# A hybrid RWKV-7/S5 block on one core: masking the chunk matrices on VectorE, and solving the two directions' triangular systems as two series

## The chip, the core and the metric

The kernel runs on one core of a Trainium2 chip. The metric is device time in microseconds (us). The kernel before takes 2064.58 us, the median of three runs (2061.06 to 2066.1). Names used below: PE is TensorE (matmuls; PEld its weight loads), DVE is VectorE, ACT is ScalarE, POOL is GpSimd, SP is the engine whose queue issues nearly all DMAs. Each engine executes its own instructions strictly in the order in which they stand in its queue, and SP's DMAs are issued in their order as well: a DMA that waits for its data holds all that stand behind it.

## The reference, cut to what matters

The model has two layers. Layer 0 mixes the tokens (256 context tokens and 512 latent ones, 768 in all) with eight bidirectional RWKV-7 heads and, beside them, 32 S5 groups; layer 1 uses latent attention; each layer ends in a mixture of experts. The change touches layer 0's mixer alone. Its core is this recurrence, for both directions z and each head:

```python
def _rwkv_step(S, inp):
    r, w, k, v, kk, a = inp
    sa = jnp.einsum('zbhvk,zbhk->zbhv', S, kk)
    S = S * w[..., None, :] - sa[..., None] * (a * kk)[..., None, :] + v[..., None] * k[..., None, :]
    return S, jnp.einsum('zbhvk,zbhk->zbhv', S, r)
```

After it each token's output is normalised per head, gets a bonus term and a gate, and is concatenated with the S5 output; then `o_l = cat @ w_out` follows. The per-layer modulation rows (`silu(c) @ mod_w[layer] + mod_b[layer]`) are a separate product over 25 MB of weights for each layer.

## The kernel before, in words

The recurrence is computed in chunks of 64 tokens. The six tiles of 128 tokens are visited in six turns s = 0 to 5 (forward direction in one order, backward in another), and each turn has two steps of one chunk for each direction. Four pieces of code make up a turn, called in `rwkv` (line 1841 and on):

- **Stage a** (`rwkv_stage_a`) loads a turn's r, k and normalised k (`rk`, from `qbuf` and `kkd`), evaluates decay and gate polynomials on ACT, POOL and DVE (`sg`, `ta`, `vv`, `ev`, `od`), scans the decays on DVE (`E`), and forms the operands `PQ` and `KB` on DVE, `ev` and `ta` products on POOL. Its last DVE instruction is `KB<-ta,E` of the second direction.
- **Stage b** (`rwkv_stage_b`) forms the chunk matrices. Per direction z and chunk parity par, PE multiplies `KB` with `PQ` into two PSUM tiles `pg`; ACT copies them to `G` in SBUF (line 570), POOL multiplies `G` with the triangular mask `gmask` (line 571). The 16x16 diagonal blocks go by DMA to DRAM (`nt`, 16 DMAs of 4 per z and par) and come back as rows `A` with one block per partition: 128 partitions hold 2 directions x 2 parities x 4 blocks x 8 heads. On them DVE inverts all blocks by forward substitution: 15 rounds of two instructions, `xt<-X,A` and `X<-X,xt`, 30 in a chain in which each needs the one before (lines 589 to 592). The inverse goes out (`xo`) and back (`D`, 16 DMAs). PE and ACT then merge 16-blocks into 32-blocks (`pd`, with the DVE addition `G<-D,pd`, 8 instructions) and into 64-blocks (`pt`, `Tb`, ACT `G<-pt`).
- **Steps** (`rwkv_steps`) run the chunk recurrence: PE products `pU`, ACT copies `R` and `VU`, PE `pZ` and `pY`, DVE scales the state (`Z<-Z,dc`) and adds (`Z<-pZ,Z`, two instructions per step). `Y` goes to DRAM as `yd`.
- **S5 runs** (`s5_run`, 16 of them in eight pairs, `S5N` says how many pairs stand behind each turn): a table `s5tq` is loaded, PE forms `s5S`, DVE rotates and scans (`s5t`, `s5G`), POOL rotates back (`s5t`, `s5H`), PE forms `s5y`, ACT and DVE apply the activation (`s5g`, `zt`); after each second pair the gate follows (`s5zT`). `s5t` and `s5G` have one buffer each.

The calls stand in the order steps(s), stage b(s+1), stage a(s+2), S5 pairs. The framework's list scheduler places all instructions at build time: what was written earlier has priority, an instruction takes its place in an engine's queue when the scheduler's own clock finds its inputs ready. `G`, `KB`, `VU` and the operand tiles have two or three buffers, `A`, `X`, `xt`, `D16`, `W16` one.

From turn 3 on, other work joins. `rwkv_out` finishes the output tiles 0 and 1 (written in turn 3), 3 and 4 (turn 4), 2 and 5 (turn 5): gate product `pgate`, POOL `vo<-vo,bsum` and `vo<-vo,lnb`, DVE `yo<-yo,yo` (the two directions added), statistics, and three more products, then a store to `rwbuf`; its buffers exist once, so one tile follows another. `mod_part(1, q)` computes layer 1's modulation rows for q = 0, 1, 2: 16 weight tiles `mw` of 512 KB each, three buffers, PE `psmod` into one PSUM tile, which DVE reads (`mo`) before the next q starts. The buffers of both lie where stage a's pool was, which is closed after stage a(5) is done. Behind the loop, `concat` reads `rwbuf` back (`cy`), PE transposes it (`ptcat`), and the output projection (`po`, weights `wo`) starts; its PSUM comes free when the last `pgate` has been read.

## Time and profile before

| | |
|---|---|
| median of three runs | 2064.58 us (2061.06 to 2066.1) |
| the profiled execution: time, span | 2061.18 us, 2059.5 us |
| granted TensorE clock, mean | 0.857 |
| PE, PEld, DVE, ACT, POOL busy | 79%, 56%, 61%, 37%, 38% of the span |

The profile is one execution, recorded by hardware. "Busy" is the time in which an engine had at least one instruction under way; two that overlap count once. The page divides the span in 40 slices; the loop described above takes from about 340 us to 900 us, slices 7 to 18, where none of the engines is busy throughout:

```profile
PE   3688996667777857648798999948899998789993
DVE  3799825895767765434654655485567754566544
ACT  4221324332533523212313545423445433326552
POOL 0576804662553541101524234360314233414432
```

### The profile page before, as it was taken

The page shows a single profiled execution, that of the slowest core. Times are in us where ns is not written, and L with a number is a line of the kernel's source. Part 1 is how long each engine was busy: PE and PEld are TensorE (multiplying, and loading weights), DVE is VectorE, ACT ScalarE, POOL GpSimd, SP SyncE. Part 2 cuts the span into 40 slices and gives each one's busy share as a digit, 9 for nine tenths or more (in the row PEclk, how much of TensorE's full clock was granted, in tenths as well). Part 3 has the DMA queues.
Part 4 walks back from the last instruction along what each step waited for, and adds up shares of the span by engine and source line. Part 5 has one row for each costly group of instructions (what it writes and reads, how often), then busy time and mean ns, then how long its engine had stood idle before and what let it go on. Part 6 is the DMA issues. An engine that isn't in the chain of part 4 may idle for free. (4 is left out here: it accounts for less than half of the span.)

```text
span 2059.5 us, 32386 instructions
## 1 busy us (share of the span) xinstructions
PE 1634.8 (79%) x12499; PEld 1156.0 (56%) x12499; DVE 1252.1 (61%) x2353; ACT 768.6 (37%) x1374; POOL 775.8 (38%) x732
## 2 busy tenths in 40 slices
PE   3688996667777857648798999948899998789993
PEld 2376766556666744326666666547445544666662
DVE  3799825895767765434654655485567754566544
ACT  4221324332533523212313545423445433326552
POOL 0576804662553541101524234360314233414432
PEclk9698998558867967768899999969799999899997
DMA  8654697532323227775615999860000005539974
GB/s 233 190 170 149 201 284 206 152 97 71 110 57 110 79 73 217 232 233 183 250 42 172 388 360 352 287 203 3 0 0 0 1 1 221 230 103 353 387 238 174
DMA packets 232581, 350.79 MB, mean 170 GB/s; under 512 B 57794, under 2 KB 178552, under 8 KB 217576
## 3 DMA queue, kind: packets, MB, share of 16 engines
q1 hardware_dynamic: 208944, 297.89, 43.3%
q0 software_dynamic: 10080, 44.04, 6.0%
q10 hardware_dynamic: 13400, 6.75, 1.2%
q8 instruction: 100, 1.64, 0.3%
q14 instruction: 57, 0.47, 0.1%
HBM read 280.60 MB, written 68.03 MB: 169 GB/s over the span
## 5 line engine op out<-in xcount | busy, mean ns | idle before, releaser
L163 PE MATMUL psmod<-mw,cst 128*32 128x256 f32 x768 | 79.9, 488 | 50.1 <-DMA mw<-in_mod_w_dram 49.6
L1754 PE MATMUL po<-P,vv 128*64 128x512 f32 x192 | 99.3, 622 | 0.8 <-ACT P L1751 0.4
L189 PE MATMUL pwi<-aT,wih 128*128 128x512 f32 (+1 forms) x224 | 83.0, 372 | 12.0 <-DVE q L329 12.0
L1751 ACT ACTIVATE P<-st 128x512 f32<-128x512 f32 x96 | 57.2, 597 | 94.3 <-PE st L1749 92.6
L571 POOL TENSOR_TENSOR G<-G,gmask 128x1024 f32<-128x1024 f32 x24 | 59.6, 2486 | 80.9 <-ACT G L570 80.7
L191 PE MATMUL pwi<-aT,wil 128*128 128x256 f32 (+1 forms) x224 | 81.4, 364 | 0.0
L190 PE MATMUL pwi<-aT,wih 128*128 128x256 f32 (+1 forms) x224 | 81.2, 363 | 0.0
L1079 PE MATMUL s5y<-s5tq,s5H 128*96 128x128 f32 x256 | 54.7, 365 | 30.5 <-POOL s5H L1071 19.9
L1760 POOL TENSOR_TENSOR sum<-sum,P 128x512 f32<-128x512 f32 x48 | 62.4, 1301 | 41.3 <-ACT P L1751 41.1
L1758 POOL TENSOR_TENSOR sum<-P,P 128x512 f32<-128x512 f32 x16 | 20.7, 1313 | 140.3 <-ACT P L1751 140.3
L1382 POOL DMA_INDIRECT xg<-fbuf,rk x36 | 37.5, 1043 | 94.5 <-PE ptx L229 56.7
L163 PEld LDWEIGHTS psmod<-mw,cst 128*32 128x32 f32 x768 | 19.8, 123 | 91.8 <-DMA mw<-in_mod_w_dram 67.2
L183 ACT ACTIVATE xT<-ptx 128x512 fp32r<-128x512 f32 x72 | 41.2, 596 | 66.7 <-PE ptx L229 66.3
L567 PE MATMUL pg<-PQ,KB 64*128 64x128 f32 x384 | 53.5, 365 | 14.2 <-ACT ta L496 9.7
L1079 PEld LDWEIGHTS s5y<-s5tq,s5H 128*96 128x96 f32 x256 | 43.7, 225 | 36.1 <-POOL s5H L1071 22.3
L1725 DVE TENSOR_REDUCE mxp<-sc 128x1 f32<-128x512 f32 x64 | 43.1, 685 | 29.5 <-PE sc L1724 29.0
L184 DVE TENSOR_TENSOR xT<-ptx,xT 128x512 fp32r<-128x512 f32 x72 | 48.1, 687 | 19.9 <-ACT xT L183 19.0
L189 PEld LDWEIGHTS pwi<-aT,wih 128*128 128x128 f32 x224 | 46.9, 211 | 22.7 <-issue 13.3
L567 PEld LDWEIGHTS pg<-PQ,KB 64*128 64x128 f32 x384 | 45.8, 256 | 21.8 <-ACT ta L496 10.0
L728 POOL TENSOR_TENSOR vo<-vo,bsum 128x512 f32<-128x512 f32 x6 | 6.2, 1042 | 133.3 <-DMA vo<-vtok 125.7
L229 PEld LDWEIGHTS ptx<-ident,xg 128*128 128x128 f32 x288 | 41.1, 193 | 27.1 <-issue 20.7
L229 PE MATMUL ptx<-ident,xg 128*128 128x128 f32 x288 | 43.0, 285 | 11.5 <-issue 7.0
(1564 smaller groups left out, 5258.1 us busy)
## 6 DMA issues: line engine op xcount, KB each, us to landing
mw<-in_mod_w_dram SPq DMA_DIRECT2D x96, 512.0 KB
yb<-yo SPq DMA_DIRECT2D x36, 512.0 KB
s5tq<-s5t SPq DMA_DIRECT2D x16, 960.0 KB
yb<-zrow SPq DMA_DIRECT2D x16, 512.0 KB
wi<-in_hy_w_in_dram SPq DMA_DIRECT2D x14, 512.0 KB
rk<-qbuf SPq DMA_DIRECT2D x12, 512.0 KB
fbuf<-f SPq DMA_DIRECT2D x10, 512.0 KB
s5t<-s5CP SPq DMA_DIRECT2D x4, 1152.0 KB
```

The costliest lines, as they stand in the source:

```text
L163: nc.tensor.matmul(ps[32 * j:32 * j + 32, 256 * h:256 * h + 256], self.cst[:, k, :], wt[:, j], start=(k == 0 and h == 0), stop=(k == 7), s ...
L184: nc.vector.tensor_tensor(lo, src, hi.bitcast(F32), OP.subtract)
L189: nc.tensor.matmul(out, lh, rh, start=start, stop=False, **kw)
L190: nc.tensor.matmul(out, lh, rl, start=False, stop=False, **kw)
L191: nc.tensor.matmul(out, ll, rh, start=False, stop=stop, **kw)
L229: nc.tensor.transpose(pt[:, k * 128:(k + 1) * 128], a[:, h * 4 + k::8], self.ident)
L567: nc.tensor.matmul(pg[hp][:, m], KB[rs, m, ps2], PQ[rs, m, ps2], start=True, stop=True, skip_group_check=True)
L571: nc.gpsimd.tensor_tensor(G[:, par], G[:, par], self.mask[:, z, par, None, :].to_broadcast([128, 8, 128]), OP.mult)
L1079: nc.tensor.matmul(out, H[:, g, d, k, h0:h0 + 96], CP[:, k, d, i0:i0 + 8, :].rearrange("p a b -> p (a b)"), start=False, stop=(d == 1 and ...
L1751: nc.scalar.activation(P, st, AF.Exp, scale=SCALE)
L1754: nc.tensor.matmul(po[64 * x:64 * x + 64], vv[:, kt, h0 + x, :], P, start=(kt == 0), stop=(kt == 5), skip_group_check=True)
L1760: nc.gpsimd.tensor_tensor(sums[x], sums[x], P, OP.add)
```

## The change

Four edits, all in the loop of layer 0. First, DVE multiplies `pg` in PSUM with the mask and writes `G`, in place of ACT's copy and POOL's multiplication. Second, the DRAM tiles `nt` and `xo` exist once per direction; `A` is loaded, `X` is stored and `D` fetched per direction, and each round of the substitution is two instructions on 64 partitions for each direction in place of two on 128. Third, `rwkv_stage_b` returns the last instruction of the substitution, and stage a(s+2) and the S5 pairs written behind it are traced in `tc.issue_after(...)`: their DVE instructions may not stand ahead of that last instruction in DVE's queue (other engines are not held). Fourth, S5 runs and their gate are given a priority 800 places later than they were written (`S5LATE`).

```diff
@@ -4,7 +4,7 @@
 
 
 import math
-from contextlib import ExitStack
+from contextlib import ExitStack, nullcontext
 
 import concourse.bacc as _bacc
 import concourse.bass as bass
@@ -44,6 +44,7 @@
 S5N = (1, 2, 2, 2, 1, 0, 0)
 MS14 = (4, 0, 5, 1, 6, 2, 7, 3, 12, 8, 9, 10, 11, 13)
 MODT = "lo"
+S5LATE = -800
 MODN = {3: (0,), 4: (1,), 5: (2,)}
 
 
@@ -550,9 +551,9 @@
 
         nc = self.nc
         f = lambda x: x.rearrange("p a b -> p (a b)")
-        nt, xo = (self.dr.tile([128, 256], F32, name=f"{n}{s}") for n in ("nt", "xo"))
-
-        units = [(z, par, q) for z in range(2) for par in range(2) for q in range(4)]
+        nt, xo = ([self.dr.tile([64, 256], F32, name=f"{n}{s}{z}") for z in range(2)] for n in ("nt", "xo"))
+
+        units = [(par, q) for par in range(2) for q in range(4)]
         unit = lambda d, u: dap(d, u * 8 * 256, [[16, 16], [256, 8], [1, 16]])
         for z in range(2):
             PQ, KB, dc = st[z]
@@ -567,12 +568,11 @@
                         nc.tensor.matmul(pg[hp][:, m], KB[rs, m, ps2], PQ[rs, m, ps2], start=True, stop=True,
                                          skip_group_check=True)
                 for hp in range(2):
-                    nc.scalar.activation(G[:, par, hp::2], pg[hp], AF.Copy)
-                nc.gpsimd.tensor_tensor(G[:, par], G[:, par], self.mask[:, z, par, None, :].to_broadcast([128, 8, 128]), OP.mult)
-                for u, (uz, up, q) in enumerate(units):
-                    if (uz, up) == (z, par):
-                        c = 64 - 64 * par + 16 * q
-                        nc.sync.dma_start(unit(nt, u), G[c:c + 16, par, :, c:c + 16])
+                    nc.vector.tensor_tensor(G[:, par, hp::2], pg[hp], self.mask[:, z, par, None, :].to_broadcast([128, 4, 128]),
+                                            OP.mult)
+                for q in range(4):
+                    c = 64 - 64 * par + 16 * q
+                    nc.sync.dma_start(unit(nt[z], units.index((par, q))), G[c:c + 16, par, :, c:c + 16])
             for par in range(2):
                 pt = self.psum("tp", f"pkt{z}{s}{par}", 1)
                 for m in range(4):
@@ -582,19 +582,24 @@
         A = wp.tile([128, 16, 16], F32, name=f"A{s}", tag="A", bufs=1)
         X = wp.tile([128, 16, 16], F32, name=f"X{s}", tag="X", bufs=1)
         tmp = wp.tile([128, 64], F32, name=f"xt{s}", tag="xt", bufs=1)
-        nc.sync.dma_start(f(A), nt)
-        nc.scalar.activation(X, self.xid, AF.Copy)
+        half = [slice(64 * z, 64 * z + 64) for z in range(2)]
+        for z, p in enumerate(half):
+            nc.sync.dma_start(f(A)[p], nt[z])
+            nc.scalar.activation(X[p], self.xid[p], AF.Copy)
         for r in range(15):
             m, n = r + 1, 15 - r
             tm = tmp[:, :m * n].rearrange("p (a b) -> p a b", b=n)
-            nc.vector.tensor_tensor(tm, X[:, 0:m, r:r + 1].to_broadcast([128, m, n]),
-                                    A[:, r:r + 1, m:16].to_broadcast([128, m, n]), OP.mult)
-            nc.vector.tensor_tensor(X[:, 0:m, m:16], X[:, 0:m, m:16], tm, OP.add)
-        nc.sync.dma_start(xo, f(X))
+            for p in half:
+                nc.vector.tensor_tensor(tm[p], X[p, 0:m, r:r + 1].to_broadcast([64, m, n]),
+                                        A[p, r:r + 1, m:16].to_broadcast([64, m, n]), OP.mult)
+            for p in half:
+                last = nc.vector.tensor_tensor(X[p, 0:m, m:16], X[p, 0:m, m:16], tm[p], OP.add)
         D, W = self.D16, self.W16
-        for u, (z, par, q) in enumerate(units):
-            c = 64 - 64 * par + 16 * q
-            nc.sync.dma_start(D[c:c + 16, z, :, 16 * (q % 2):16 * (q % 2) + 16], unit(xo, u))
+        for z, p in enumerate(half):
+            nc.sync.dma_start(xo[z], f(X)[p])
+            for u, (par, q) in enumerate(units):
+                c = 64 - 64 * par + 16 * q
+                nc.sync.dma_start(D[c:c + 16, z, :, 16 * (q % 2):16 * (q % 2) + 16], unit(xo[z], u))
         kw = dict(start=True, stop=True, skip_group_check=True)
 
         B = [[(32 * g, z, h) for g in range(4)] for z in range(2) for h in range(8)]
@@ -636,6 +641,7 @@
         for par in range(2):
             for z in range(2):
                 nc.scalar.activation(st[z][2][one[par], par, :, two[par]], ps[one[par], z], AF.Copy)
+        return last.ins
 
     def rwkv_state(self, rp):
         nc = self.nc
@@ -1863,19 +1869,22 @@
                 q0 = next(pairs)
                 if q0 % 4 == 0:
                     zt[0] = w5.tile([96, 8, 128], F32, name=f"zt{q0}", tag="zt", bufs=1)
-                self.s5_run(q0, zt[0], w5)
-                if q0 % 4 == 2:
-                    self.s5_glu(q0 // 4, zt[0], lambda m, z: nc.sync.dma_start(s5d[m], z), w5)
+                with self.tc.high_priority(S5LATE):
+                    self.s5_run(q0, zt[0], w5)
+                    if q0 % 4 == 2:
+                        self.s5_glu(q0 // 4, zt[0], lambda m, z: nc.sync.dma_start(s5d[m], z), w5)
 
         self.rwkv_stage_b(0, st[0], sp, gp, wp)
         s5(S5N[0])
         for s in range(6):
             self.rwkv_steps(s, st[s], wp)
+            behind = nullcontext()
             if s < 5:
-                self.rwkv_stage_b(s + 1, st[s + 1], sp, gp, wp)
-            if s < 4:
-                st[s + 2] = self.rwkv_stage_a(s + 2, sp, wa)
-            s5(S5N[s + 1])
+                behind = self.tc.issue_after(self.rwkv_stage_b(s + 1, st[s + 1], sp, gp, wp))
+            with behind:
+                if s < 4:
+                    st[s + 2] = self.rwkv_stage_a(s + 2, sp, wa)
+                s5(S5N[s + 1])
             if s in (1, 2):
                 self.zero_blocks(z0, s - 1)
             if s == 3:
```

**DVE, substitution of turn 2.** Before (left in its place among `X`, `xt`, the rows `od`, `wseg`, `E` are stage a(3), `X_5138` is turn 2's):

```order
L592 TENSOR_TENSOR X_5138<-X_5138,xt_5139 128x6x10
L513 SCALAR_TENSOR_TENSOR wseg_2691<-ev_5529,od_5535 128x8x64
L514 SCALAR_TENSOR_TENSOR wseg_2692<-ev_5529,od_5535 128x8x64
L590 TENSOR_TENSOR xt_5139<-X_5138,A_5137 128x63
L521 SCALAR_TENSOR_TENSOR E_5543<-wseg_2691,one_2704 128x520
L521 SCALAR_TENSOR_TENSOR E_5545<-wseg_2692,one_2704 128x520
L592 TENSOR_TENSOR X_5138<-X_5138,xt_5139 128x7x9
L535 TENSOR_TENSOR PQ_5549<-rk_5503,E_5543 128x4x128
L536 TENSOR_TENSOR PQ_5549<-rk_5503,E_5543 128x4x2x64
L528 COPY dc_5547<-E_5545 128x8
L590 TENSOR_TENSOR xt_5139<-X_5138,A_5137 128x64
```

After, the same stretch (`X_5198` is turn 2's; the second direction's last rows and what follows them):

```order
L593 TENSOR_TENSOR xt_5199<-X_5198,A_5197 64x15
L596 TENSOR_TENSOR X_5198<-X_5198,xt_5199 64x15
L508 TENSOR_TENSOR od_5628<-od_5628,vv_5621 128x512
L509 SCALAR_TENSOR_TENSOR od_5628<-od_5628,vv_5621 128x512
L510 SCALAR_TENSOR_TENSOR od_5628<-od_5628,sg_5599 128x512
L514 SCALAR_TENSOR_TENSOR wseg_2691<-ev_5622,od_5628 128x8x64
L515 SCALAR_TENSOR_TENSOR wseg_2692<-ev_5622,od_5628 128x8x64
L522 SCALAR_TENSOR_TENSOR E_5636<-wseg_2691,one_2704 128x520
L522 SCALAR_TENSOR_TENSOR E_5638<-wseg_2692,one_2704 128x520
L536 TENSOR_TENSOR PQ_5642<-rk_5596,E_5636 128x4x128
L537 TENSOR_TENSOR PQ_5642<-rk_5596,E_5636 128x4x2x64
L701 TENSOR_TENSOR Z<-pZ_4964,Z 64x8x64 x2
```

The rows of stage a(3) that stood between the rounds now follow the last round. In the rows ahead of these, turn 2's first direction runs through its 30 instructions before the second begins; this is so in turns 2, 3, 4 and 5, while in turns 0 and 1 the two directions alternate.

**DVE, the end of the loop.** Before, from the first step of turn 5 (`yo_9005` is output tile 2):

```order
L695 TENSOR_TENSOR Z<-pZ_8855,Z 64x8x64 x2
L664 TENSOR_TENSOR Z<-Z,dc_7557 128x512
L664 TENSOR_TENSOR Z<-Z,dc_7616 128x512
L695 TENSOR_TENSOR Z<-pZ_8954,Z 64x8x64 x2
L181 SCALAR_TENSOR_TENSOR cat_9203<-cz_9207,cat_9202 128x768
L181 SCALAR_TENSOR_TENSOR cat_9203<-cz_9211,cat_9202 128x768
L736 TENSOR_TENSOR yo_9005<-yo_9005,yo_9006 128x512
L739 TENSOR_REDUCE mu_9010<-yo_9005 128x8
L740 TENSOR_SCALAR mu_9010<-mu_9010 128x8
```

After, from the first step of turn 5 (`yo_7935` is output tile 0, `yo_7972` tile 1; tiles 3, 4, 2 and 5 follow in this order):

```order
L736 TENSOR_TENSOR vo_7929<-vo_7929,pgate_7926 128x512
L737 TENSOR_TENSOR gw_7928<-lnw,pgate_7926 128x512
L755 TENSOR_TENSOR yo_7935<-yo_7935,gw_7928 128x512
L756 TENSOR_TENSOR yo_7935<-yo_7935,vo_7929 128x512
L729 TENSOR_SCALAR gd_8801<-gd_8801 128x128
L701 TENSOR_TENSOR Z<-pZ_9140,Z 64x8x64 x2
L729 TENSOR_SCALAR gd_8838<-gd_8838 128x128
L736 TENSOR_TENSOR vo_7966<-vo_7966,pgate_7963 128x512
L737 TENSOR_TENSOR gw_7965<-lnw,pgate_7963 128x512
L742 TENSOR_TENSOR yo_7972<-yo_7972,yo_7973 128x512
L745 TENSOR_REDUCE mu_7977<-yo_7972 128x8
```

In the queue before, tiles 0, 1, 3 and 4 stand ahead of the last `Z<-pZ`, and tiles 2 and 5 behind it; after, tile 0 alone stands ahead, and five tiles behind.

**SP, the substitution's DMAs of turn 5.** In both orders they stand among layer 1's loads of `mw`. Before, turn 5's fetches `D` of both directions (`xo_8152`, stored five rows further up; `Y_7962` is turn 4's first step, `yo_7817` output tile 1):

```order
L161 DMA mw_7930<-in_mod_w_dram 128x4x256
L721 DMA gd_8652<-qbuf 128x128
L161 DMA mw_7936<-in_mod_w_dram 128x4x256
L597 DMA D_2698<-xo_8152 16x8x16 x3
L161 DMA mw_7942<-in_mod_w_dram 128x4x256
L597 DMA D_2698<-xo_8152 16x8x16 x3
L734 DMA yo_7817<-yd_2712 128x512
L701 DMA yd_2712<-Y_7962 64x512
L701 DMA yd_2713<-Y_7962 64x512
L597 DMA D_2698<-xo_8152 16x8x16 x10
```

After, from the output of turn 4's second step on (`Y_8216`; `xo_8309` is turn 5's second direction, whose first direction was stored and fetched further up):

```order
L707 DMA yd_2712<-Y_8216 64x512
L707 DMA yd_2713<-Y_8216 64x512
L162 DMA mw_8898<-in_mod_w_dram 128x4x256
L162 DMA mw_8904<-in_mod_w_dram 128x4x256
L162 DMA mw_8910<-in_mod_w_dram 128x4x256
L154 DMA gm_9256<-in_norm_g_dram 2x512
L599 DMA xo_8309<-X_8403 64x256
L162 DMA mw_8916<-in_mod_w_dram 128x4x256
L162 DMA mw_8922<-in_mod_w_dram 128x4x256
L602 DMA D_2698<-xo_8309 16x8x16 x8
```

The fetches `D` stood on both sides of the `yd` of turn 4's first step; now the second direction's stand behind that of the second step, with its store `xo_8309` and loads of `mw` between them. Its load `A_8402` stands behind the first step's `yd`.

## Rows read from the trace of the kernel before

**Rows 1.** Engines in three stretches; columns us, busy us (instructions), granted clock, DMA share, GB/s.

```profile
340.00:480.00 140.00, 78.06 (x1010) 68.64 (x1008) 114.74 (x182) 54.83 (x126) 82.66 (x70) 0.59 0.49 139
480.00:720.00 240.00, 185.65 (x3714) 158.37 (x3716) 168.59 (x338) 104.56 (x223) 112.55 (x123) 0.82 0.30 88
720.00:900.00 180.00, 119.93 (x2276) 77.98 (x2274) 91.34 (x195) 41.94 (x78) 39.50 (x40) 0.73 0.61 185
```

**Rows 2.** DVE, timeline, second half: start us, us, engine, instruction [idle <-releaser].

```profile
717.57 1.38 DVE L695 TENSOR_TENSOR Z<-pZ,Z 64x512 f32<-64x512 f32 x2
...
746.96 0.67 DVE L545 TENSOR_TENSOR KB<-ta,E 128x512 f32<-128x512 f32 x1
...
762.35 1.65 DVE L736 TENSOR_TENSOR yo<-yo,yo 128x512 f32<-128x512 f32 x1 [1.46 <-DMA yo<-yd]
...
775.50 1.50 DVE L617 TENSOR_TENSOR G<-D,pd 32x256 f32<-32x256 f32 x4
...
803.74 1.39 DVE L695 TENSOR_TENSOR Z<-pZ,Z 64x512 f32<-64x512 f32 x2 [3.82 <-PE pZ L693]
...
828.84 1.38 DVE L695 TENSOR_TENSOR Z<-pZ,Z 64x512 f32<-64x512 f32 x2
...
847.96 2.26 DVE L617 TENSOR_TENSOR G<-D,pd 32x256 f32<-32x256 f32 x6
...
882.65 1.39 DVE L695 TENSOR_TENSOR Z<-pZ,Z 64x512 f32<-64x512 f32 x2 [1.56 <-PE pZ L693]
...
895.15 1.39 DVE L695 TENSOR_TENSOR Z<-pZ,Z 64x512 f32<-64x512 f32 x2 [9.78 <-PE pZ L693]
```

**Rows 3.** The end: DVE's adds for output tiles 2 and 5, PE's first `po`.

```profile
907.95 0.69 DVE L736 TENSOR_TENSOR yo<-yo,yo 128x512 f32<-128x512 f32 x1 [2.50 <-DMA yo<-yd]
...
922.29 1.61 DVE L736 TENSOR_TENSOR yo<-yo,yo 128x512 f32<-128x512 f32 x1 [4.81 <-DMA yo<-yd]
...
937.49 1.22 PE L189 MATMUL po<-wo000hi,cat 128*128 128x512 f32 x2 [0.78 <-ACT wo000hi L183]
```

**Rows 4.** Tile `Z`: all instructions of a line; ns min/median/max, first and last start us.

```profile
L664 DVE TENSOR_TENSOR Z<-Z,dc x24: 676/691/2843, 347.6 to 884.7; 128x512 f32<-128x512 f32 x24
L695 DVE TENSOR_TENSOR Z<-pZ,Z x24: 653/689/695, 485.4 to 895.8; 64x512 f32<-64x512 f32 x24
```

**Rows 5.** The old copy (line 570) and mask (line 571) of `G`, in the same form.

```profile
L570 ACT ACTIVATE G<-pg x48: 574/597/598, 372.0 to 771.8; 128x512 f32<-128x512 f32 x48
...
L571 POOL TENSOR_TENSOR G<-G,gmask x24: 2336/2362/2851, 377.6 to 772.5; 128x1024 f32<-128x1024 f32 x24
```

**Rows 6.** The substitution's first line, in the same form.

```profile
L590 DVE TENSOR_TENSOR xt<-X,A x90: 142/210/2269, 411.3 to 794.0; 128x15 f32<-128x15 f32 x12, 128x28 f32<-128x28 f32 x12, 128x39 f32<-128x39 f32 x12, 128x48 f32<-128x48 f32 x12
```

**Rows 7.** DVE's timeline, first, middle and last rows of turn 4's substitution.

```profile
704.06 0.56 DVE L590 TENSOR_TENSOR xt<-X,A 128x15 f32<-128x15 f32 x1
...
715.77 0.21 DVE L590 TENSOR_TENSOR xt<-X,A 128x60 f32<-128x60 f32 x1
715.90 0.68 DVE L545 TENSOR_TENSOR KB<-ta,E 128x512 f32<-128x512 f32 x1
...
743.68 0.18 DVE L590 TENSOR_TENSOR xt<-X,A 128x15 f32<-128x15 f32 x1
743.89 0.18 DVE L592 TENSOR_TENSOR X<-X,xt 128x15 f32<-128x15 f32 x1
```

**Rows 8.** Tile `s5t` alone, the loop; columns PE, PEld, DVE, POOL, clock, DMA share, GB/s.

```profile
340.00:900.00 560.00, 0.00 (x0) 0.00 (x0) 61.50 (x160) 77.54 (x96) 0.73 0.45 132
```

**Rows 9.** SP's queue: first `mw` of layer 1, turn 5's `xo` and last `D`.

```profile
761.15 2.18 SPq L161 DMA_DIRECT2D mw<-in_mod_w_dram  x3
...
797.35 0.50 SPq L593 DMA_DIRECT2D xo<-X  x1
...
813.67 4.86 SPq L597 DMA_DIRECT2D D<-xo  x10
```

**Rows 10.** Tile `mw`, layer 1's 48 loads, in the form of rows 4.

```profile
L161 SPq DMA_DIRECT2D mw<-in_mod_w_dram x48: 367/396/1657, 761.2 to 905.2; - x48
```

## The prediction

> **What bounds the kernel now.** I read the busy slices first, then the loop's stretches, then DVE's timeline, waits last. In the loop no engine is the bound: in 340 to 900 us DVE is busy 114.74 + 168.59 + 91.34 = 374.7 of 560 us, POOL 234.7, ACT 201.3 [rows 1]. It is a chain that crosses engines and DMA. DVE is nearest to being full, 82% up to 480 us, 70% up to 720, and 51% after. So I cut the loop where turn 3's last state addition starts, 717.6 us [rows 2]: up to there DVE sets the pace, behind it the chain of turns 4 and 5 (`D`, merges, steps) with a half idle DVE, and behind the last state addition (895.15) a tail of its own: tiles 2 and 5 are finished one after the other, their adds 14.3 us apart (907.95, 922.29), and the first `po` follows 15.2 us after the second (937.49) [rows 3]. What is behind `po` is untouched by the diff, so the end shifts as the last tile's add shifts.
>
> **The change part by part.**
>
> *Masks.* 48 DVE instructions of 512 elements from PSUM are added. DVE's nearest row is the state addition, also 512 elements with a PSUM operand: 0.69 us, longest 0.695 [rows 4]. 48 x 0.69 = 33 us on DVE. ACT loses 48 x 0.597 = 29, POOL 24 x 2.36 = 57 [rows 5], neither of which is full; per half of a turn the way from `pg` to `G` gets shorter by one POOL instruction. POOL's masks read SBUF while DVE does; `Z<-Z,dc`, whose operands both lie in SBUF, has a median of 0.691 but a maximum of 2.843, while the addition from PSUM is never stretched [rows 4]. So DVE gets back something between 0 and the 57 us of the masks; with DVE busy two thirds of the time (374.7 of 560) and not all of it of the stretched kind I take 36, of which 30 lie before 717 us.
>
> *Two series.* 30 more instructions in each of six turns, 180 at the median of 0.21 [rows 6] = 38 us if each waits for the one before, 23 if the directions alternate, since an independent instruction starts 0.13 us after the one ahead of it (715.77, 715.90) [rows 7]. The order alternates in turns 0 and 1 alone; I take 38, 32 of it before turn 3's last addition. Against it, the series is no longer spread: turn 4's runs from 704.06 to 743.9 with other work between its rounds [rows 7]; two directions back to back, at 0.22 from one start to the next, are 60 x 0.22 = 13 us. In the new order it stands ahead of turn 3's first step's addition.
>
> [...]
>
> *Stage a and S5 behind the series.* No instruction is added. Sixteen runs cost DVE 61.5 and POOL 77.5 us on `s5t` [rows 8], 3.8 and 4.8 each. Counting runs in DVE's queue, fifteen stand ahead of turn 3's last addition before, nine after: 6 x 3.84 = 23 us of DVE and 29 of POOL go to the last part, which has 49% and 78% of 180 us idle [rows 1]. Stage a(5) goes the other way: its last `KB`, at 746.96 now [rows 2], stands in the new order right behind the cut, and the rest of its stage ahead of it, some 8 us of DVE work by the instructions counted there. It frees the room of `rwkv_out` and of `mw`, whose first load starts at 761.15 [rows 9]; 14 us from `KB` to there, so about 733 after.
>
> *First part, sum.* DVE is busy 283 us of the 380 up to 720 (114.74 + 168.59), and waits 97. After: 283 + 29 (42 of the masks) + 32 + 8 - 23 - 30 = 299. The waits contain those for POOL's mask and for the interleaved series; if they all stay, the cut is at 734, if they shrink by 30 at 704. I take 81, and the cut at 718, where it is now.
>
> *Second part.* Now 717.57 to 895.15, 177.6 us [rows 2]. `G<-D` of turn 4 starts at 775.5; its series ended at 743.9, so 31.6 later. After, the series is over before the cut, but `G<-D` still stands behind tile 0's work, which takes 13.2 us (762.35 to 775.50) and starts with its loads after stage a(5): about 740. From there the distances of before: 28.2 to the first addition of turn 4 (768; I take 770 for the six S5 runs), 25.1 to the second, in which tile 1 stood with some 7 us of DVE work that is now gone: 18, so 788. Then turn 5's second direction: its `xo` stands behind that step's `yd` and loads of `mw` (797), its `D` come some 15 us later, as now from 797.35 to 813.67 [rows 9], 812; another 15 for `pd` and the S5 runs ahead of it on DVE, which wait for POOL: `G<-D` at 827, 21 before today's 847.96. Then 34.7 + 12.5 as now [rows 2], less 1: last addition at 873, 22 us earlier.
>
> *Tail.* Ahead of the last addition tile 0 alone is finished, no longer 0, 1, 3 and 4. Tile 1 starts when the queue reaches it, and the buffers exist once, so five tiles follow each other, at the 14.3 us of rows 3. DVE's share of one tile is nine instructions of 512 elements at 0.69 [rows 3] and some small ones, about 7 us; the rest are waits for loads and for ACT and POOL, so the idle DVE doesn't hide it. Before, the last add lies 27 us behind the last addition (922.3 - 895.2); after, 4 x 14.3 + about 4 = 61. So 873 + 61 = 934, against 922.3: +12. The layer 1 loads, 48 from 761.2 to 905.2 [rows 10], some 3.1 us apiece, start about 28 us earlier and end before that, so they don't set the end.
>
> Sum: the profiled execution has 2061.2, which is 3.4 below the median of the runs (2064.6). 2061.2 + 12 = 2073, and 2076 as the median. The point of no change is a last addition at 861, 34 us earlier than now.
>
> **The rivals.**
>
> A, faster: DVE's waits really shrink. For: POOL's mask and the spread series both leave the chain, and the second part gives DVE work to do while it waits. Against: the second part is paced by DMA round trips. If the cut comes at 704 and turn 5's `xo` isn't held (its `G<-D` then 15 after the second addition, as the earlier turn), the last addition is at about 845, the last add at 906, -16: 2045 profiled, 2048 as the median.
>
> B, slower by SP's queue: turn 5's second `A` and `xo` stand behind `yd` of turn 4's steps and behind loads of `mw` that wait for their three buffers. Where PE gets to `psmod` late (it executes in order, behind turn 4's steps), each load holds `xo`. Up to ten loads at 3.1 us [rows 10] stand between; with all of them in the path and the series itself late, turn 5's `G<-D` is not before 850 and the last addition at 900: last add 961, +39, 2103. It decides from turn 4's second step on. For: the same queue holds `D` in three pieces today, between 797 and 818 [rows 9].
>
> C, the change does not do what it says in the tail: PE, ACT or POOL instructions of tiles 1, 3 and 4 stand early and only DVE's part is late, so the five follow at 10 us, half way between DVE's 7 and 14.3: 17 us less, -5, about 2059. I count it within the forecast's own range.
>
> **How the numbers follow.** Forecast with C 0.47, its own range 2059 to 2092; A 0.36; B 0.17. A measurement of this kernel can tell about 0.3%, 6.2 us, from no change. Of the forecast's 0.47, C's side gives 0.03 to faster and 0.16 to no change, 0.28 to slower; A gives 0.33 to faster and 0.03 to the same; B all of 0.17 to slower. Faster 0.36, same 0.19, slower 0.45. The unknown costs are the relief (0 to 57), the waits (30 either way) and the spacing of the tiles (10 to 14.3). A range from 2038 to 2106 reaches past A and B and leaves out 2 in 10: a relief of the whole 57 us below, tiles and SP late together above.
>
> **What would show it.** `G<-pg` on DVE at 0.69; POOL without `gmask`; turn 4's series in under 15 us and before turn 3's last addition. Turn 3's last addition at 704 to 734; the last of turn 5 at 873. Behind it five adds `yo<-yo,yo`, 14 us apart, while DVE is mostly idle, and `po` 15 us behind the fifth. Wrong it is if the last addition comes before 855 (A) or after 885 (B shows `xo` of turn 5 late on SP), or if the five tiles follow in much under 14 us.

## The result and the profile after

The changed kernel takes 2071.67 us (median of 15 runs) beside 2059.53 us of the kernel before (15 runs); the ratio is 1.0052, 95% interval 1.0037 to 1.0068: slower by half a per cent. One of the changed kernel's runs took 5072 us, for a reason not found, and is left out of the ratio. Forecast were 2076 us and +0.55%. The profiled execution has 2079.11 us, span 2077.3; it is one of the longer ones, 7 us above the median, and 17.9 us above the profiled execution before, where the medians differ by 12.1.

The stretches of [rows 1] in the changed kernel (columns as there: us, busy and instructions of PE, PEld, DVE, ACT, POOL, granted clock, DMA share, GB/s):

```profile
340.00:480.00 140.00, 84.44 (x1022) 73.00 (x1020) 117.16 (x259) 50.53 (x122) 55.76 (x55) 0.59 0.49 137
480.00:720.00 240.00, 167.88 (x3418) 142.84 (x3418) 171.41 (x402) 88.85 (x199) 59.19 (x67) 0.77 0.24 67
720.00:900.00 180.00, 139.04 (x2628) 96.89 (x2624) 106.12 (x264) 41.73 (x74) 51.89 (x84) 0.86 0.73 228
```

DVE is busy 20 us more than before, POOL 68 less, ACT 20 less. DVE's timeline at the marks of [rows 2], here with the last `KB` of stage a(5), tile 0's add, turn 4's and 5's `G<-D` and the state additions from turn 3's second step on:

```profile
724.35 1.39 DVE L701 TENSOR_TENSOR Z<-pZ,Z 64x512 f32<-64x512 f32 x2
726.40 1.05 DVE L546 TENSOR_TENSOR KB<-ta,E 128x512 f32<-128x512 f32 x1 [0.66 <-POOL ta L545]
...
736.72 0.69 DVE L742 TENSOR_TENSOR yo<-yo,yo 128x512 f32<-128x512 f32 x1 [0.78 <-DMA yo<-yd]
...
746.02 2.27 DVE L622 TENSOR_TENSOR G<-D,pd 32x256 f32<-32x256 f32 x6 [1.81 <-PE pd L618]
...
780.15 1.39 DVE L701 TENSOR_TENSOR Z<-pZ,Z 64x512 f32<-64x512 f32 x2 [0.94 <-PE pZ L699]
...
799.71 0.68 DVE L701 TENSOR_TENSOR Z<-pZ,Z 64x512 f32<-64x512 f32 x1 [0.48 <-PE pZ L699]
...
831.62 3.06 DVE L622 TENSOR_TENSOR G<-D,pd 32x256 f32<-32x256 f32 x8 [0.57 <-PE pd L618]
...
854.15 1.38 DVE L701 TENSOR_TENSOR Z<-pZ,Z 64x512 f32<-64x512 f32 x2
...
870.42 1.39 DVE L701 TENSOR_TENSOR Z<-pZ,Z 64x512 f32<-64x512 f32 x2 [3.83 <-PE pZ L699]
```

Turn 3's addition is 7 us later than before, the last one 25 us earlier. Behind it stand the five adds of tiles 1, 3, 4, 2 and 5, and PE's first `po` (compare [rows 3]):

```profile
879.18 0.69 DVE L742 TENSOR_TENSOR yo<-yo,yo 128x512 f32<-128x512 f32 x1 [2.52 <-DMA yo<-yd]
...
895.31 1.34 DVE L742 TENSOR_TENSOR yo<-yo,yo 128x512 f32<-128x512 f32 x1 [4.06 <-DMA yo<-yd]
...
911.22 1.69 DVE L742 TENSOR_TENSOR yo<-yo,yo 128x512 f32<-128x512 f32 x1 [4.67 <-DMA yo<-yd]
...
925.70 1.38 DVE L742 TENSOR_TENSOR yo<-yo,yo 128x512 f32<-128x512 f32 x1 [4.83 <-DMA yo<-yd]
...
939.68 1.38 DVE L742 TENSOR_TENSOR yo<-yo,yo 128x512 f32<-128x512 f32 x1 [5.00 <-DMA yo<-yd]
```
```profile
954.14 1.22 PE L190 MATMUL po<-wo000hi,cat 128*128 128x512 f32 x2 [0.78 <-ACT wo000hi L184]
```

They lie 14 to 16 us apart, each waiting for its loads. `po` starts 16.7 us later than before, and the profiled execution is 17.9 us longer: nearly all that this execution loses is there when `po` starts. The 25 us that the loop gained are outweighed by 42 that the tail became longer (69.3 from the last addition to the last add, against 27.1). Two questions are left: what brought the last addition forward, and why the tiles stand behind it.

The second can be read from PE's timeline in the changed kernel, around the first gate product:

```profile
857.52 1.12 PE L1115 MATMUL s5gl<-s5zT,s5glu 128*128 128x512 f32 x2
...
860.88 1.13 PE L731 MATMUL pgate<-gup,gd 128*128 128x512 f32 x2
```

`pgate` of tile 0 starts 2 us behind the last gate product of the S5 runs. Both use the one PSUM buffer `s5a`, which goes round in the order in which the code is written, and all S5 runs are written ahead of the tiles. Their priority 800 places later would therefore hold back every tile (`a_pgate` below tests this): tile 0's `gw` and `vo` must wait for `pgate`, and tile 1 must wait for tile 0's buffers.

### The profile page after: what moved, and what is told of

Read it like the earlier page. It is cut to its first block, busy times and chain, and to the rows that moved or that the text cites. A ratio compares the mean times of both kernels' runs of the same rounds, so it can differ in the third digit from the quotient of the medians.

```text
span 2077.3 us, 32584 instructions
## 1 busy us (share of the span) xinstructions
PE 1636.3 (79%) x12499; PEld 1159.0 (56%) x12499; DVE 1273.5 (61%) x2581; ACT 745.8 (36%) x1332; POOL 714.3 (34%) x708
## 5 line engine op out<-in xcount | busy, mean ns | idle before, releaser
L164 PE MATMUL psmod<-mw,cst 128*32 128x256 f32 x768 | 74.0, 461 | 30.5 <-DMA mw<-in_mod_w_dram 28.6
L1071 POOL TENSOR_TENSOR s5t<-s5G,s5tq 128x384 f32<-128x384 f32 x16 | 17.2, 1072 | 158.8 <-issue 99.7
L1764 POOL TENSOR_TENSOR sum<-P,P 128x512 f32<-128x512 f32 x16 | 20.8, 1315 | 137.9 <-ACT P L1757 137.9
L593 DVE TENSOR_TENSOR xt<-X,A 64x15 f32<-64x15 f32 (+7 forms) x180 | 44.6, 248 | 33.9 <-DMA A<-nt 28.6
L190 PEld LDWEIGHTS pwi<-aT,wih 128*128 128x128 f32 x224 | 47.3, 212 | 23.5 <-issue 14.3
```

The costliest lines, as they stand in the source:

```text
L164: nc.tensor.matmul(ps[32 * j:32 * j + 32, 256 * h:256 * h + 256], self.cst[:, k, :], wt[:, j], start=(k == 0 and h == 0), stop=(k == 7), s ...
L190: nc.tensor.matmul(out, lh, rh, start=start, stop=False, **kw)
L593: nc.vector.tensor_tensor(tm[p], X[p, 0:m, r:r + 1].to_broadcast([64, m, n]), A[p, r:r + 1, m:16].to_broadcast([64, m, n]), OP.mult)
```

## Experiments

Ratios are to the kernel before, run on the same chip in the same job; 95% intervals in brackets. Times of marks are from one profile of each.

**Two buffers for the tiles, in both kernels** (`a_out2` is the changed kernel, `b_out2` the kernel before):

```diff
-        tl = lambda n: wp.tile([128, 512], F32, name=f"{n}{t}", tag=n, bufs=1)
+        tl = lambda n: wp.tile([128, 512], F32, name=f"{n}{t}", tag=n, bufs=1 if n == "gw" else 2)
```

> The changed kernel, with two buffers in place of one for yo (both), and vo in the work on the output tiles (gw keeps one). Two tiles now stand ahead of the last state addition in DVE's queue and four behind it. Theory T (the loss is the tail: each tile behind the last state addition waits for the one before it to leave its buffers, 15.1 us apart in the changed kernel's profile): the loads go ahead, tiles follow at 8 to 10 us, last addition still at about 871 us, last add at 871 + 9 + 3 x 9 = 907, 15 us earlier than the kernel before: ratio about 0.993. Rival S (the distance of tiles is set by their chain over PE, ACT and POOL and by the single gw, not by the loads): 15 us stay, last add at 925, ratio 1.000 to 1.002.

> The kernel before with the same two buffers. Only two tiles stand behind the last state addition there, so theory T expects at most one distance to shrink, 5 us: ratio 0.997 to 1.000. If the gain is as large as in the changed kernel (15 us or more), it is not the number of tiles behind the last addition that counts, and T falls.

Measured: the changed kernel 0.9948 [0.9929, 0.9967], 2050.48 us, last addition 883.0, last add 910.7; the kernel before 0.9922 [0.9896, 0.9948], 2044.42 us. In the first the tail shrank from 69 to 28 us, as T expects, since tiles come in pairs; the last addition came 13 us later, which T didn't expect. In the second the gain is 16 us, three times what T allowed, and by the line drawn there T falls as it was put: it is not the number of tiles behind the last addition alone that costs. Where else, the adds of tiles 3 and 4 show, first in the kernel before, then with two buffers (this profiled execution, at 2037.64 us, is 7 us under the median of its kernel):

```profile
841.77 0.69 DVE L736 TENSOR_TENSOR yo<-yo,yo 128x512 f32<-128x512 f32 x1 [4.98 <-DMA yo<-yd]
...
860.90 0.69 DVE L736 TENSOR_TENSOR yo<-yo,yo 128x512 f32<-128x512 f32 x1 [8.44 <-DMA yo<-yd]
```
```profile
834.91 0.69 DVE L736 TENSOR_TENSOR yo<-yo,yo 128x512 f32<-128x512 f32 x1
836.24 3.06 DVE L617 TENSOR_TENSOR G<-D,pd 32x256 f32<-32x256 f32 x8
839.41 0.68 DVE L736 TENSOR_TENSOR yo<-yo,yo 128x512 f32<-128x512 f32 x1
...
861.16 1.39 DVE L695 TENSOR_TENSOR Z<-pZ,Z 64x512 f32<-64x512 f32 x2 [3.23 <-PE pZ L693]
...
874.77 1.39 DVE L695 TENSOR_TENSOR Z<-pZ,Z 64x512 f32<-64x512 f32 x2 [4.07 <-PE pZ L693]
...
888.42 1.39 DVE L736 TENSOR_TENSOR yo<-yo,yo 128x512 f32<-128x512 f32 x2 [3.79 <-DMA yo<-yd]
```

With two buffers DVE no longer waits for their loads (13 us for the two before); they are 4.5 us apart in place of 19, the last addition is at 874.8 in place of 895.2, and the last two adds follow at once, 14 us behind it. In the kernel before, the late loads of tiles 3 and 4 (4.98 and 8.44 us of waiting) stop the steps behind them in DVE's queue just as those of tiles 2 and 5 (2.50 and 4.81 us, [rows 3]) stop the end.

**The tiles alone, moved** (`b_tail5`: the kernel before, with tiles 1, 3 and 4 held behind the last addition on DVE; as their code is written behind turn 5 for that, their work on the other engines and their loads have a later place as well):

```diff
-                nc.vector.tensor_tensor(Z[hp, :, :, hp], pZ[hp], Z[hp, :, :, hp], OP.add)
+                self.zlast = nc.vector.tensor_tensor(Z[hp, :, :, hp], pZ[hp], Z[hp, :, :, hp], OP.add)
...
-            for t in {3: (0, 1), 4: (3, 4), 5: (2, 5)}.get(s, ()):
-                self.rwkv_out(t, op, rwd)
+            if s == 3:
+                self.rwkv_out(0, op, rwd)
+            if s == 5:
+                with self.tc.issue_after(self.zlast.ins):
+                    for t in (1, 3, 4, 2, 5):
+                        self.rwkv_out(t, op, rwd)
```

> The kernel before, with one thing changed: the output tiles 1, 3 and 4 are held behind the last state addition in DVE's queue, as they stand in the changed kernel; masks, substitution and S5 runs as before. Theory D (the changed kernel's last state addition comes 25 us earlier because the tiles no longer stand among the steps, not because of masks, series or late S5 runs): last addition at 868 to 878, last add 69 us later, 937 to 947: ratio 1.007 to 1.012. Rival O (the change's own edits bring the last addition forward): last addition stays at 886 to 896, last add 955 to 965, ratio 1.016 to 1.021.

Measured: 1.0117 [1.0096, 1.0138], 2083.74 us. DVE's marks:

```profile
776.46 3.10 DVE L617 TENSOR_TENSOR G<-D,pd 32x256 f32<-32x256 f32 x8
...
803.03 1.39 DVE L695 TENSOR_TENSOR Z<-pZ,Z 64x512 f32<-64x512 f32 x2 [4.68 <-PE pZ L693]
...
814.75 1.38 DVE L695 TENSOR_TENSOR Z<-pZ,Z 64x512 f32<-64x512 f32 x2
836.06 3.06 DVE L617 TENSOR_TENSOR G<-D,pd 32x256 f32<-32x256 f32 x8 [18.60 <-PE pd L613]
...
874.35 1.39 DVE L695 TENSOR_TENSOR Z<-pZ,Z 64x512 f32<-64x512 f32 x2 [7.40 <-PE pZ L693]
...
941.88 1.46 DVE L736 TENSOR_TENSOR yo<-yo,yo 128x512 f32<-128x512 f32 x1 [4.78 <-DMA yo<-yd]
```

Both marks fall into theory D's ranges. Moving the tiles, with masks, series, edge and S5 runs as before, brings the last addition forward by 20.8 us (895.15 to 874.35) of the changed kernel's 24.7, and the last add back by 19.6 (922.29 to 941.88). If the two add, the earlier end of the loop in the changed kernel is thus for the most part the same event as its longer tail. And beside a kernel with the same displacement the change is a gain: 1.0052 over 1.0117 is 0.9936, some 13 us, where the medians differ by 12. The two profiles show only 2 of them up to the last add (939.7 against 941.9), and 3 in the whole execution (2079.1 against 2082.2), for the one lies 7 us above the median of its runs and the other 2 below; where the rest lies was not found.

**The gate product out of the S5 runs' buffer** (`a_pgate` the changed kernel, `b_pgate` the one before, `a_pgate_out2` the changed one with two tile buffers as well):

```diff
-        pg = self.psum("s5a", f"pgate{t}", 1)
+        pg = self.psum("gr", f"pgate{t}", 2)
```

> The changed kernel, with the gate product pgate of the output tiles in the PSUM buffers of pg (two, free between two turns' chunk matrices) in place of the one that the S5 runs and their gate use (s5a). In the changed kernel's trace the first pgate starts at 860.9, 2 us behind the last S5 gate product, and the first tile cannot finish before it. Theory P (the late S5 runs hold pgate through the shared PSUM buffer, and that is why five tiles stand behind the last state addition): with its own place the first pgate starts before 790, four tiles stand ahead of the last addition and two behind; last addition 870 to 885, last add 27 us later, 897 to 912: 10 to 25 us under the kernel before, ratio 0.988 to 0.995. Rival Q (tiles among the steps cost the loop what the tail saves): last addition back at 895 or later, ratio 1.000 to 1.005.

> The kernel before with the same move of pgate. There the S5 runs were nearly done when the tiles began (first pgate 793.4). Theory P: little to gain, 0 to 8 us, ratio 0.996 to 1.000. If it gains as much as the changed kernel does, P falls as the reason for the five tiles behind.

> The changed kernel with pgate moved and two buffers for yo and vo. Theory P with two buffers: what each gives adds in part: last addition 865 to 880, two tiles behind it in 18 us, last add 883 to 898: ratio 0.981 to 0.988. Rival Q: not better than the two buffers alone (0.995).

Measured: `a_pgate` 1.0002 [0.9977, 1.0026], `b_pgate` 0.9978 [0.9952, 1.0004], `a_pgate_out2` 0.9953 [0.9928, 0.9979]. The second is in theory P's range, the first and the third are in rival Q's. In `a_pgate` PE and DVE show:

```profile
734.05 3.60 PE L731 MATMUL pgate<-gup,gd 128*128 128x512 f32 x4
```
```profile
757.70 0.69 DVE L742 TENSOR_TENSOR yo<-yo,yo 128x512 f32<-128x512 f32 x1 [0.23 <-DMA nt<-G]
...
897.56 1.39 DVE L701 TENSOR_TENSOR Z<-pZ,Z 64x512 f32<-64x512 f32 x2 [2.14 <-PE pZ L699]
...
904.95 0.69 DVE L742 TENSOR_TENSOR yo<-yo,yo 128x512 f32<-128x512 f32 x1
...
919.01 1.48 DVE L742 TENSOR_TENSOR yo<-yo,yo 128x512 f32<-128x512 f32 x1 [4.90 <-DMA yo<-yd]
```

The cause of the order is P's: `pgate` starts at 734 in place of 861, tile 1's add at 757.7 in place of 879.2, and two tiles stand behind the last addition. P's ranges for the last addition, the last add and the ratio are missed, as Q expected: the last addition is back at 897.6, and the tail's gain is spent. But the reason that Q gave, tiles among the steps, is not shown, since the move puts `pg` of turn 5 behind `pgate` of tiles 0 and 1 in the same two buffers: turn 5's last mask ran at 791.2, and at 774.3 in the changed kernel. `a_pgate_out2`, whose tiles have two buffers, speaks for the masks: its last addition is at 895.1 all the same, and turn 5's last mask ran at 797.6. How much of the 27 us the tiles cost isn't told apart, and a PSUM buffer of its own for `pgate` was not tried.

**The S5 runs early** (`a_s5early`) **and no edge** (`a_noissue`):

```diff
-S5LATE = -800
+S5LATE = 0
```
```diff
-                behind = self.tc.issue_after(self.rwkv_stage_b(s + 1, st[s + 1], sp, gp, wp))
+                self.rwkv_stage_b(s + 1, st[s + 1], sp, gp, wp)
```

> The changed kernel with the S5 runs at their own priority (no 800 places later). DVE's queue has four tiles ahead of the last state addition and two behind, as the kernel before. Theory T: the last addition may come some 10 us later than in the changed kernel (880, since S5 work is back in the crowded part) but the tail is 27 us, last add 907 to 910: ratio 0.993. Rival L (the late S5 runs are what brought the last addition forward by 25 us): last addition back at 895, last add 922, ratio 1.000.

> The changed kernel without the edge that keeps stage a and S5 behind the substitution on DVE. Four tiles behind the last state addition. Theory T: last addition between 871 and 885, last add 54 us later, 925 to 939: ratio 1.002 to 1.009. Rival L2 (the edge is what costs, because stage a's operands come late): ratio 0.995 or lower with a last addition before 865.

Measured: 1.0039 [1.0021, 1.0056] and 1.016 [1.013, 1.0189]. With early S5 runs four tiles stand ahead, as T expected, but the last addition is at 908.5 (880 expected), the last add at 929.6 (907 to 910), and the ratio is 1.0039 (0.993): T's numbers fail, and rival L's (895, 922, 1.000) are nearer. Late S5 runs and displaced tiles together are worth about as much as they cost. Without the edge both of T's ranges are missed, and L2's too: the last addition comes at 895.6 and the last add at 955.8, with 60 us behind it where 54 were expected. Turn 4's substitution then runs from 701.6 to 755.7, its two series spread among stage a's instructions again; in the changed kernel it is over at 697.6. Of the three edits that were taken out of the changed kernel one at a time (edge, late S5 runs, and two series in `a_joint` below), the edge is thus the only one whose loss clearly cost time; the masks were not taken out.

**The masks alone** (`b_mask`, the kernel before with the first edit; the diff is that of line 570) **and with two tile buffers** (`b_mask_out2`):

> The kernel before with the masks alone on DVE (from PSUM, in place of ACT's copy and POOL's mask). By the sum of the prediction DVE gets 33 us and gets back some 36 from POOL's silence, and POOL's 2.4 us per half leave the way from pg to G: ratio 0.996 to 1.004, last addition 888 to 900. Rival M (the masks alone bring the last addition forward, as the whole change did by 25 us): last addition at 870 to 880, ratio 0.988 to 0.993. Rival N (DVE has no room): last addition 905 or later, ratio 1.005 or more.

> The kernel before with the masks on DVE and two buffers for yo and vo of the output tiles. If the two add (masks 0.9985, buffers 0.9922): 0.988 to 0.992. If they take the same waits away: 0.992 to 0.996.

Measured: 0.9985 [0.9964, 1.0006], last addition 895.7: as the sum had it, DVE gives about what it gets. It is busy 368.7 us from 340 to 900, 6.0 less than before; with 48 x 0.688 = 33.0 us of masks added, some 39 came back. That is the end, not the marks between: turn 3's last addition is at 735.4 (717.6 before), turn 4's first `G<-D` at 757.4 (775.5).

With two buffers the ratio is 0.9988 [0.9975, 1.0001], above both ranges: beside the masks the buffers' gain of 0.8% is gone. The last addition is at 896.1 there (874.8 with the buffers alone). The traces show where it stays: turn 5's last mask, and the start of its series. First `b_out2`'s masks on POOL, then `b_mask_out2`:

```profile
L571 POOL TENSOR_TENSOR G<-G,gmask x24: 2337/2370/2857, 378.4 to 764.6; 128x1024 f32<-128x1024 f32 x24
```
```profile
L570 DVE TENSOR_TENSOR G<-pg,gmask x48: 659/683/693, 372.7 to 801.3; 128x512 f32<-128x512 f32 x48
```
```profile
812.96 0.72 DVE L590 TENSOR_TENSOR xt<-X,A 128x15 f32<-128x15 f32 x1 [2.96 <-DMA A<-nt]
```

With work on the tiles and `mo` between these masks on DVE, turn 5's last one starts 37 us later, the series starts 38 us later (774.9 in `b_out2`), and `G<-D` of turn 5 follows at 856.4 in place of 836.2. All profiles taken here fit this: in the six in which turn 5's last mask starts by 778, the last addition comes at 870 to 883, but at 895.2 in the kernel before, with its single-buffered tiles among the steps; in the eight in which it starts at 791 or later, the last addition comes at 895 or later, whatever was done about the tiles. No run moves these masks alone, so this is read from the traces and not shown by an experiment.

**One series again** (`a_joint`: the changed kernel with `nt`, `xo`, `A`, `X` and `D` for both directions together and 30 instructions a turn):

> The changed kernel with the substitution again as one series on 128 partitions (nt, xo, A, X, D for both directions together); masks on DVE, the edge for stage a and S5, and the late S5 runs as in the changed kernel. One tile more stands ahead of the last state addition, four behind. Theory (two series cost DVE 30 instructions a turn, 6 us, on the path in most turns, as the prediction's 38 us says): turn 3's last addition 15 to 30 us earlier than the changed kernel's 724, last of turn 5 at 850 to 865, ratio 0.992 to 1.001. Rival (the split pays, since the first direction's round trip through DRAM runs beside the second's series): last additions no earlier than in the changed kernel, 724 and 870 or later, ratio 1.003 or more.

Measured: 1.0057 [1.0033, 1.0082]. Turn 3's last addition came 27 us earlier (697.2), as the theory had it; but the last of turn 5 is at 874.3, later than in the changed kernel, and the last of four tiles behind it adds at 931.9, so that the theory's end and its ratio are missed and the rival's are met. With the split the first part takes 27 us more, and none of that is left at the end of the loop.

**The edge on the kernel before with two buffers** (`b_edge_out2`: one series, masks on ACT and POOL, S5 early):

```diff
-                self.rwkv_stage_b(s + 1, st[s + 1], sp, gp, wp)
-            if s < 4:
-                st[s + 2] = self.rwkv_stage_a(s + 2, sp, wa)
-            s5(S5N[s + 1])
+                behind = self.tc.issue_after(self.rwkv_stage_b(s + 1, st[s + 1], sp, gp, wp))
+            with behind:
+                if s < 4:
+                    st[s + 2] = self.rwkv_stage_a(s + 2, sp, wa)
+                s5(S5N[s + 1])
```

> The kernel before with two buffers for yo and vo (0.9922 alone) and the edge that keeps stage a's and S5's DVE instructions behind the last one of the substitution; masks on ACT and POOL, one series on 128 partitions, S5 at its own priority. Theory E (the edge is the useful part of the change: without it the changed kernel is 1.1% slower): series in 8 us in place of 40, turn 3's last addition 10 to 20 us earlier than 711, ratio 0.984 to 0.990. Rival (the edge only helps where two series of 64 partitions would otherwise be spread; here it delays stage a and S5): ratio 0.992 or more.

Measured: 1.0047 [1.003, 1.0064], against 0.9922 without the edge: theory E falls, the rival holds. Turn 4's series does get shorter, 18 us from 711.9 in place of 40 from 697.4, but turn 3's last addition is at 747.2 (710.9 without the edge), the last one at 912.0. The edge that helps the changed kernel by 1.1% costs this one about 1.3%. The two differ in more than the series (masks, S5 runs, buffers), and `a_joint`, one series with the edge, is no slower than the changed kernel: that the series is what decides is not shown. The fastest version is `b_out2`, the kernel before with two buffers for `yo` and `vo`: 2044.42 us, 0.8% under the kernel before, and 1.3% under the changed one.

## Why the prediction was right, point by point

**Masks.** 48 x 0.69 on DVE; measured 0.680 each (median, 0.656 to 0.693). In the form of [rows 4] the scaling of the state, whose longest before ran beside a mask on POOL (last section), and the masks:

```profile
L670 DVE TENSOR_TENSOR Z<-Z,dc x24: 666/684/1746, 351.5 to 856.2; 128x512 f32<-128x512 f32 x24
```
```profile
L571 DVE TENSOR_TENSOR G<-pg,gmask x48: 656/680/693, 378.4 to 774.3; 128x512 f32<-128x512 f32 x48
```

The longest scaling of the state fell from 2.84 to 1.75 us, and the same 160 instructions on `s5t` cost DVE 48.7 us in place of the 61.5 of [rows 8]. In `b_mask`, where the masks alone moved, they cost 50.6, so most of this is the masks' doing (here the form of [rows 8], `b_mask` first, then the changed kernel):

```profile
340.00:900.00 560.00, 0.00 (x0) 0.00 (x0) 50.61 (x160) 83.40 (x96) 0.76 0.46 137
```
```profile
340.00:900.00 560.00, 0.00 (x0) 0.00 (x0) 48.73 (x160) 74.56 (x96) 0.75 0.46 137
```

The relief can be had from the sum: 33 of masks and 38 of series were added up to 900 us, about one and a half tiles (10) went behind it, and DVE is busy 20 us more, so some 40 came back (39 in `b_mask`); 36 were taken. The waits shrank less than forecast: up to turn 3's last addition DVE is busy 292.9 of 384.4 us, and 281.0 of 377.6 before, so 12 more (16 forecast), and it waits 5 less where 16 were taken. That is why this addition is 7 us later than before.

**Two series.** 180 more instructions at a median of 0.206 (0.210 before, [rows 6]), as taken. That they run in one go was wrong. DVE's timeline of turn 4's, first and last row of each direction:

```profile
662.50 0.17 DVE L593 TENSOR_TENSOR xt<-X,A 64x15 f32<-64x15 f32 x1 [5.94 <-DMA A<-nt]
...
672.30 0.17 DVE L596 TENSOR_TENSOR X<-X,xt 64x15 f32<-64x15 f32 x1
...
688.34 0.17 DVE L593 TENSOR_TENSOR xt<-X,A 64x15 f32<-64x15 f32 x1 [3.60 <-DMA A<-nt]
...
697.45 0.18 DVE L596 TENSOR_TENSOR X<-X,xt 64x15 f32<-64x15 f32 x1
```

Each direction takes 9 to 10 us, but the second's `A` comes 16 us after the first is over: 35 us from first to last, and not the 13 that the prediction gave. It was still over before turn 3's additions, which is all that the sum used. Turn 5's second direction, first and last row and one between, does matter:

```profile
791.79 0.17 DVE L593 TENSOR_TENSOR xt<-X,A 64x15 f32<-64x15 f32 x1 [4.25 <-DMA A<-nt]
...
797.95 0.56 DVE L1055 TENSOR_TENSOR s5t<-s5S,s5tq 128x384 f32<-128x384 f32 x1
...
810.04 0.18 DVE L596 TENSOR_TENSOR X<-X,xt 64x15 f32<-64x15 f32 x1
```

It takes 18 us, since late S5 runs, a state addition and `mo` stand between its rounds: the edge holds back only what is written behind it, and these were written ahead. So turn 5's `xo` comes 13 us later than in the kernel before, and than forecast.

**S5 and stage a.** The ninth of sixteen runs starts at 713.7, the tenth at 729.9, so nine stand ahead of turn 3's last addition, as counted. The first load of layer 1's `mw` is at 736.7 (733 forecast).

**The marks.** Turn 3's last addition 724 (718 forecast, 704 to 734 the bounds); `G<-D` of turn 4 746 (740); additions of turn 4 780 and 800 (770, 788); SP's `xo` 810 and last `D` 813 (797, 812); `G<-D` of turn 5 832 (827); additions of turn 5 854 and 870 (861, 873). That 870 meets 873 is in part luck: `xo` is 13 us late, its `D` start 2.5 us behind it where 15 were taken, and from turn 5's `G<-D` to the last addition it is 38.8 us where 46.2 were taken. SP's queue held turn 5's `xo` little, against rival B:

```profile
810.25 0.47 SPq L599 DMA_DIRECT2D xo<-X  x1
810.82 1.48 SPq L162 DMA_DIRECT2D mw<-in_mod_w_dram  x2
812.74 4.53 SPq L602 DMA_DIRECT2D D<-xo  x8
```

Two loads of 1.5 us together stood in between. Rival A needed a last addition before 855 and did not come; rival C needed tiles at 10 us, and they follow at 15.1 (939.68 - 879.18 over 4), 0.8 more than the 14.3 taken.

**The tail.** 61 us forecast, 69.3 measured: 8.8 to the first add (4 taken) and four distances of 15.1. With 870 + 69 the last add is at 940 (934), and `po` 14.5 behind it. The mechanism is the one forecast; the tail is 8 us longer than forecast, the last add 6 us later, and `b_tail5` shows it without the other edits. The profiled execution is 17.9 us longer where 12 were forecast; the medians of all runs differ by less, 12.1 us, and that these meet the forecast so closely (0.52%, and 0.55% forecast) is luck.

**What the prediction had mis-sized.** It put the loop's earlier end down to the earlier `G<-D` and to 7 us of tile 1's DVE work. `b_tail5` shows that the tiles' leaving gives 21 us by itself, without an earlier `G<-D` of turn 4: 776.5 there, 746.0 in the changed kernel, and both end their loop within 4 us of each other. The 30 us by which the changed kernel is ahead there are nearly gone at turn 5's `G<-D` (831.6 against 836.1), whose `D` come from the late series above. And it is not DVE's 7 us a tile that the steps lose: between turn 4's two additions 13 us go (25.1 before, 11.7 in `b_tail5`), from turn 5's `G<-D` to the last addition 9 (47.2 before, 38.3), where the prediction took 7 and 1. The second it took "as now", though tile 4, whose add waits 8.44 us for its loads there, was to leave as well. And the order was only read, not explained: the reason, the PSUM buffer that S5 and `pgate` share, is visible in the code and in the trace.

## What to carry to other kernels

When work is moved to a lower priority, look at every buffer that it shares with what is written behind it: the rotation follows the order of the code, so late work holds back later work that has nothing to do with it. The tiles with their single buffers cost DVE waits for their loads wherever they stood in its queue: 13 us for tiles 3 and 4 among the steps of the kernel before, 21 us for the five behind the last addition of the changed one (2.52 + 4.06 + 4.67 + 4.83 + 5.00). Moving them from the middle to the end moved the cost. A second buffer gained 0.8% in the kernel before (0.9922), but not where other work came late instead (0.9988 with the masks on DVE, 1.0047 with the edge): after each such move, look again at what the last stage waits for. An earlier end of a stage is worth nothing before it is known what was moved behind it.

## What the runs showed of the hardware

Half the partitions saved next to nothing: an instruction of the substitution takes 0.206 us on 64 partitions and 0.210 on 128 (medians). The masks from PSUM on DVE took between 0.656 and 0.693 us in the changed kernel, the 13 of the 48 that ran beside an instruction on POOL no longer than the others. The scaling of `Z`, both of whose operands lie in SBUF, took 0.666 to 0.693 us wherever POOL had nothing under way; each one above 0.70, eight of 24 before and five of 24 after, ran beside an instruction on POOL. The longest before, 2.84 us, stood beside a mask:

```profile
497.97 3.45 DVE L664 TENSOR_TENSOR Z<-Z,dc 128x512 f32<-128x512 f32 x2
498.17 2.70 POOL L571 TENSOR_TENSOR G<-G,gmask 128x1024 f32<-128x1024 f32 x1 [24.57 <-ACT G L570]
```

The longest after took 1.75 us (708.24), beside `ev<-ev,vv` on POOL. Not all that ran beside POOL were longer: the one at 722.25 before took 0.68 us, with a mask on POOL from 722.37 on. On `s5t`, DVE's 160 instructions took 61.5 us before and 50.6 in `b_mask`, where the masks alone moved.
